# w_o and w_down with the tokens on the partitions, in a two-layer hybrid trunk kernel

## Chip, core and metric

One core of one Trainium2 chip. The metric is the device time of one execution in microseconds (us), median of three runs. The engines are TensorE (PE in the profile, its weight loads PEld), VectorE (DVE), ScalarE (ACT), GpSimd (POOL) and SyncE (SP), whose queue issues most DMA transfers.

## What is computed

One step of a trunk of two layers over 640 tokens of width 1024: 128 prompt tokens (chunk 0, with the modulation vector c_ctx) and 512 sample tokens (chunks 1 to 4, with c). Cut to what the change touches:

```python
h = rms_norm(x, g_pre1) * (1 + sc1) + sh1
parts = split(h @ w_in)                     # conv mixer, attention, DeltaNet, gates
ya, yb, yc = conv(parts) @ w_pa, attention(parts) @ w_pb, deltanet(parts) @ w_pc
mix = (ga * ya + gb * yb + gc * yc) @ w_o
x = x + gt1 * rms_norm(mix, g_post1)
h2 = rms_norm(x, g_pre2) * (1 + sc2) + sh2
ffn = (silu(h2 @ w_gate) * (h2 @ w_up)) @ w_down      # 2816 wide, 22 blocks of 128
x = x + gt2 * rms_norm(ffn, g_post2)
```

rms_norm divides by the root of the mean square over the 1024 features; scale, shift and gate are one vector each for prompt and sample tokens. Everything is fp32.

## The kernel before

All activations lie with the features on the partitions: x is eight tiles of 128x640 (block k of 128 features), and a product takes a 128x128 block of the weights as the stationary operand and 320 tokens (a half) as the moving one. For precision each fp32 operand is split into a high and a low part of the type fp32r, and a linear layer is three products per block (mm3, L362 to L365): high x high, high x low, low x high. Weight blocks come by SP into raw tiles of 128x4x128 (256 KB) and are split by ACT (a CAST, L94) and DVE (a subtraction, L95). linear (L394) streams a column block's weights for both halves; lin_half (L384) does one half with blocks that are kept.

The order of each engine's instructions is set by a scheduler at build time: a priority that follows the program's text, and free slots of the tile pools. Generators that are woven into each other (run, weave, L1196 to L1222) say which streams share a stretch. A stretch that cannot be interleaved is a joint: the norm after w_o, before the FFN, and the norm after w_down, before the next layer's input projection, since a norm needs all 1024 features of a token.

The joints are made by lin_res (L463 to L511). It does two column blocks by linear and keeps the weights of the last six (KEEP), so that half 0 of the tokens is finished ahead of half 1. For each block, sumsq (L141) squares the result on ACT and adds it up on DVE, and ACT multiplies by gate x gain (L479); after the last, half_rstd (L154) sums over the partitions by a product with a matrix of ones on PE (L157), and DVE multiplies by the factor (L496) and adds x (L497), which is read again from DRAM (xd, stored feature-wise by store_x, L459). Then prenorm_half (L192) does the same sums for the next norm and prenorm_apply (L168) makes the two fp32r parts of the next input: an ACT operation or cast for the high part (L183, L188) and a DVE operation for the low one (L184). That last half is run as a side stream in the lead (group, L410): the first five column blocks of the next stage, whose weights are ready ahead. w_down is cut in two: fill_down (L1223) does its first F1 = 14 of 22 blocks while the rest of the FFN goes on, into the tiles pt; lin_res adds the rest.

At the start load_x (L201) reads each chunk of 128 tokens with the tokens on the partitions and transposes it on PE (L211, copies L213); x's sums of squares are made by prenorm_sum, while PE does w_mod's first products (mod_mm, L271) from 16 + 16 tiles that load_first (L241) fetches. At the end out_half (L1228) transposes x back (L1236), copies it (L1237) and stores it (L1238).

## Time and profile before

| | |
|---|---|
| median of 3 runs | 2765.67 us (2762.79 to 2771.64) |
| profiled execution | 2771.84 us, span 2769.8 us |
| mean granted clock of TensorE | 0.99 |
| PE busy | 2704.1 us, 98% |
| PEld busy | 2585.7 us, 93% |
| DVE busy | 1564.8 us, 56% |
| ACT busy | 1256.1 us, 45% |
| DMA | 288.15 MB, 104 GB/s in the mean |
| 40 slices of 69 us | PE at 9 tenths or more in 38 of them, 7 in the first, 8 in the last |

The span runs from the first instruction to the end of the last transfer; the execution's own time is 2 us longer. Busy times are sums over instructions, and a product that waits in PE's pipeline counts as busy, so the start-to-start interval is what a product costs. The chain of waits goes back from the end to what released each step, and says which engine a shorter time must come from.

### The profile page before, as it was taken

The page shows a single profiled execution, that of the slowest core. Times are in us where ns is not written, and L with a number is a line of the kernel's source. Part 1 is how long each engine was busy: PE and PEld are TensorE (multiplying, and loading weights), DVE is VectorE, ACT ScalarE, POOL GpSimd, SP SyncE. Part 2 cuts the span into 40 slices and gives each one's busy share as a digit, 9 for nine tenths or more (in the row PEclk, how much of TensorE's full clock was granted, in tenths as well). Part 3 has the DMA queues.
Part 4 walks back from the last instruction along what each step waited for, and adds up shares of the span by engine and source line. Part 5 has one row for each costly group of instructions (what it writes and reads, how often), then busy time and mean ns, then how long its engine had stood idle before and what let it go on. Part 6 is the DMA issues. An engine that isn't in the chain of part 4 may idle for free.

```text
span 2769.8 us, 49615 instructions
## 1 busy us (share of the span) xinstructions
PE 2704.1 (98%) x19706; PEld 2585.7 (93%) x19706; DVE 1564.8 (56%) x3385; ACT 1256.1 (45%) x2863; POOL 26.6 (1%) x147
## 2 busy tenths in 40 slices
PE   7999999999999999999999999999999999999998
PEld 4899999999898999999989999999999999999997
DVE  4686575477743744224476865754777465442344
ACT  4533554466534633223455345544655364332343
POOL 0000000000000000000000000000000000000001
PEclk9999999999999999999999999999999999999999
DMA  8552355433564344444532323433233432222241
GB/s 241 74 77 54 81 91 109 84 67 96 162 165 152 123 133 150 128 154 146 171 89 62 71 50 86 96 87 88 66 96 120 130 97 83 77 71 75 81 120 60
DMA packets 387511, 288.15 MB, mean 104 GB/s; under 512 B 18666, under 2 KB 348112, under 8 KB 387280
## 3 DMA queue, kind: packets, MB, share of 16 engines
q1 hardware_dynamic: 387280, 285.00, 39.3%
q8 instruction: 154, 2.52, 0.4%
q14 instruction: 77, 0.63, 0.1%
HBM read 251.86 MB, written 33.07 MB: 103 GB/s over the span
## 4 chain that ended last, share of the span: by engine, by line
PE 82%; DVE 7%; DMA 5%; ACT 3%; issue 1%; SPq 0%; POOL 0%; DVEq 0%; ACTq 0%; POOLq 0%
PE l L363 23%; PE l L364 22%; PE l L365 22%; DMA wm<-in_w_mod_dram 1%; PE pm L324 1%; DMA wraw<-in_w_in_dram 1%; DMA rowb<-gd 1%; PE ptT L770 1%; PE po L780 1%; PE po L782 1%; PE scan L1068 1%; PE sco L363 1%; PE po L781 1%; DVE Tt L987 1%; PE scan L1076 1%
## 5 line engine op out<-in xcount | busy, mean ns | idle before, releaser
L94 ACT CAST whi<-wraw 128x512 fp32r<-128x512 f32 (+1 forms) x540 | 332.1, 616 | 837.1 <-PE l L364 786.6
L95 DVE TENSOR_TENSOR wlo<-wraw,whi 128x512 fp32r<-128x512 f32 (+1 forms) x540 | 367.3, 682 | 529.8 <-ACT whi L94 510.0
L363 PE MATMUL l<-hh,whi 128*128 128x320 f32 x1856 | 590.0, 318 | 5.7 <-ACT padc L858 3.3
L364 PE MATMUL l<-hl,whi 128*128 128x320 f32 x1856 | 583.5, 314 | 0.0
L365 PE MATMUL l<-hh,wlo 128*128 128x320 f32 x1856 | 582.7, 314 | 0.0
L363 PE MATMUL l<-h2h,whi 128*128 128x320 f32 x1248 | 387.4, 310 | 0.0
L364 PE MATMUL l<-h2l,whi 128*128 128x320 f32 x1248 | 385.3, 309 | 0.0
L365 PE MATMUL l<-h2h,wlo 128*128 128x320 f32 x1248 | 385.3, 309 | 0.0
L363 PEld LDWEIGHTS l<-hh,whi 128*128 128x128 f32 x1856 | 352.6, 190 | 9.3 <-ACT padc L858 3.5
L364 PEld LDWEIGHTS l<-hl,whi 128*128 128x128 f32 x1856 | 352.5, 190 | 2.0
L365 PEld LDWEIGHTS l<-hh,wlo 128*128 128x128 f32 x1856 | 352.7, 190 | 1.0
L363 PEld LDWEIGHTS l<-h2h,whi 128*128 128x128 f32 x1248 | 234.6, 188 | 7.0 <-ACT fs L427 3.1
L364 PEld LDWEIGHTS l<-h2l,whi 128*128 128x128 f32 x1248 | 234.6, 188 | 0.0
L365 PEld LDWEIGHTS l<-h2h,wlo 128*128 128x128 f32 x1248 | 234.6, 188 | 0.0
L363 PE MATMUL l<-ah,whi 128*128 128x320 f32 x544 | 169.0, 311 | 0.0
L364 PE MATMUL l<-al,whi 128*128 128x320 f32 x544 | 168.0, 309 | 0.0
L365 PE MATMUL l<-ah,wlo 128*128 128x320 f32 x544 | 167.9, 309 | 0.0
L363 PE MATMUL l<-rsh,whi 128*128 128x320 f32 x384 | 119.7, 315 | 0.0
L365 PE MATMUL l<-rsh,wlo 128*128 128x320 f32 x384 | 118.4, 310 | 0.0
L364 PE MATMUL l<-rsl,whi 128*128 128x320 f32 x384 | 118.3, 312 | 0.0
L363 PEld LDWEIGHTS l<-ah,whi 128*128 128x128 f32 x544 | 102.2, 188 | 2.2 <-issue 1.3
L364 PEld LDWEIGHTS l<-al,whi 128*128 128x128 f32 x544 | 102.3, 188 | 0.0
(427 smaller groups left out, 5310.3 us busy)
## 6 DMA issues: line engine op xcount, KB each, us to landing
wraw<-in_w_in_dram SPq DMA_DIRECT2D x256, 256.0 KB
wm<-in_w_mod_dram SPq DMA_DIRECT2D x80, 512.0 KB
wraw<-in_w_gate_dram SPq DMA_DIRECT2D x88, 256.0 KB
...
```

Of the source, the lines that this page charges most:

```text
L94: A.copy(hi, src)
L95: V.tensor_sub(lo, src, hi.bitcast(F32))
L324: T.matmul(pm[32 * u:32 * u + 2, 0:256], lhsT=sc[:, k, :], rhs=w[:, u * 256:(u + 1) * 256], start=(n == 0), stop=(n == KD - 1))
L363: T.matmul(out, lhsT=wh, rhs=ah, start=first, stop=False)
L364: T.matmul(out, lhsT=wh, rhs=al, start=False, stop=False)
L365: T.matmul(out, lhsT=wl, rhs=ah, start=False, stop=last)
L770: T.transpose(pt[:, i, q * P:(q + 1) * P], sm_[q][:, kt * P:(kt + 1) * P], ident)
L780: T.matmul(po, lhsT=vh, rhs=th, start=(kt == 0), stop=False)
L781: T.matmul(po, lhsT=vl, rhs=th, start=False, stop=False)
L782: T.matmul(po, lhsT=vh, rhs=tl, start=False, stop=(kt == 4))
L987: V.tensor_add(Tt[:, j + 1:32, 0:j], Tt[:, j + 1:32, 0:j], tv)
L1068: T.matmul(pst[:, 1, :], lhsT=XT[h, d][:, c, :], rhs=r, start=True, stop=True)
```

## The change

w_o and the second part of w_down are computed by nat_res with the tokens on the partitions: the stationary operand is now a 128x128 block of activations (128 features, one chunk of 128 tokens) and the moving one a row block of the weights, 128x512 (wrow: one transfer of 2 KB per partition). A layer is done in two groups of 512 columns. nat_stream does the first for all five chunks, k block by k block, in five banks of PSUM; the second group's split weight rows are kept meanwhile and then used chunk by chunk: chunks 0, 1, 2, then 3 and 4 interleaved. Now a token's features lie along the free axis: the sum of squares is an ACT operation with an accumulated output (sqsum), the factor a 128x1 column (tok_rstd), gate x gain is a row broadcast to all partitions (gr, made once per layer and stored in DRAM), and the residual one DVE operation. x is kept in DRAM token-wise (xd) and stored by ACT's queue. For the next stage x must come back to features on the partitions: the norm's factor is put on the diagonal of a 128x128 matrix (diag), and a full fp32 product of x's block with it transposes and scales at once (pre_t); gain and shift, four by ACT and four by DVE, the CAST of 128x8x128 and the subtraction follow. rest() does this for chunks 3 and 4 within the lead. Lead weights are split ahead in the second group (ahead). load_x uses the same diagonal products in place of transposes, and the output of the last layer is stored as it is, without transposes. fill_down uses nat_stream for both column groups; F1 is 15; the rope table lies in two C slots; the two fp32r halves of an input are two tiles of 128x8x640 (hpair).

The core of the diff:

```diff
     def load_x(c):
         xn = sb.tile([P, D], F32, tag="E", name="xn", bufs=3)
-        src = I["x_prompt"][0] if c == 0 else I["x_sample"][0, (c - 1) * P:c * P]
-        SY.dma_start(out=xn, in_=src)
+        SY.dma_start(out=xn, in_=xin(c))
         if c == 0:
             SY.dma_start(out=rows2[0:8], in_=vrow(I["c"][0]))
             SY.dma_start(out=rows2[8:16], in_=vrow(I["c_ctx"]))
+        st = small("st0", (P, 2), 3)
+        for g in range(2):
+            sqsum(st[:, g:g + 1], q4(xn[:, g * 512:(g + 1) * 512]))
+        tok_rstd(st)
+        dg = diag(st[:, 0:1])
         for g in range(2):
             pt = bank("xt")
             for j in range(4):
-                T.transpose(pt[:, j * P:(j + 1) * P], xn[:, (4 * g + j) * P:(4 * g + j + 1) * P], ident)
+                T.matmul(pt[:, j * P:(j + 1) * P], lhsT=xn[:, (4 * g + j) * P:(4 * g + j + 1) * P], rhs=dg, start=True, stop=True)
             for j in range(4):
-                (A.copy if j % 2 else V.tensor_copy)(xs[4 * g + j][:, c * P:(c + 1) * P], pt[:, j * P:(j + 1) * P])
+                (A.copy if j % 2 else V.tensor_copy)(xs[4 * g + j][:, TS[c]], pt[:, j * P:(j + 1) * P])
...
+        pt = bank("gr")
+        T.transpose(pt[0:16, 0:P], gsc[l][g[0]].rearrange("p k s -> p (k s)"), ident)
+        gr = half("gr")[0:16, 0:P]
+        A.copy(gr, pt[0:16, 0:P])
+        A.dma_start(out=gsd[l, g[0]].rearrange("k s p -> (k s) p"), in_=gr)
...
+    def wrow(srcw, k, g, keep=None):
+        raw = sb.tile([P, 4, P], F32, tag="wr", name="wraw", bufs=NWR)
+        SY.dma_start(out=raw.rearrange("p a b -> p (a b)"), in_=srcw[k * P:(k + 1) * P, g * 512:(g + 1) * 512])
+        hi, lo = wsplit(raw, [P, 4, P], keep)
+        return hi.rearrange("p a b -> p (a b)"), lo.rearrange("p a b -> p (a b)")
+    def mmn(out, act, c, wh, wl, first, last):
+        ah, al = act
+        T.matmul(out, lhsT=ah[:, TS[c]], rhs=wh, start=first, stop=False)
+        T.matmul(out, lhsT=ah[:, TS[c]], rhs=wl, start=False, stop=False)
+        T.matmul(out, lhsT=al[:, TS[c]], rhs=wh, start=False, stop=last)
...
+    def nat_stream(srcw, acts, g, ev):
+        pbs = [bank("nl"), bank("nl")] + [lbank() for _ in range(3)]
+        for k, a in enumerate(acts):
+            wh, wl = wrow(srcw, k, g)
+            for c in range(5):
+                mmn(pbs[c], a, c, wh, wl, k == 0, k == len(acts) - 1)
+                if k == len(acts) - 1:
+                    ev(c, pbs[c])
+            yield 3.2
...
-    def lin_res(srcw, acts, ys, gs, keeps, part, after, xe, end=False):
...
...
+    def nat_res(srcw, acts, gd_, xsrc, ydst, part, X, L, nrm, side=iter(()), ahead=iter(())):
...
+        def post(c, g, pb):
+            src = q4(pb)
+            if part:
+                src = u[c, g]
+                V.tensor_add(src, src, q4(pb))
+            else:
+                u[c, g] = ptile(c, g)
+            sqsum(st[:, c, g:g + 1], src)
+            V.tensor_mul(u[c, g], src, gr[int(c == 0)][g])
+            if g:
+                tok_rstd(st[:, c, 0:2])
+        def post_x(c):
+            for g in range(2):
+                V.scalar_tensor_tensor(out=u[c, g], in0=u[c, g], scalar=st[:, c, 0:1], in1=xt[c][:, 4 * g:4 * g + 4, :],
+                                       op0=ALU.mult, op1=ALU.add)
+                if nrm is None:
+                    SY.dma_start(out=q4(ydst(c))[:, 4 * g:4 * g + 4], in_=u[c, g])
+            if nrm is not None:
+                for g in range(2):
+                    sqsum(st[:, c, 2 + g:3 + g], u[c, g])
+                for g in range(2):
+                    A.dma_start(out=q4(ydst(c))[:, 4 * g:4 * g + 4], in_=u[c, g])
+            load_xt(c + 2)
+        def pre(c):
+            tok_rstd(st[:, c, 2:4])
+            dg[c] = diag(st[:, c, 2:3])
+        def pre_t(c):
+            gs, sh = nrm
+            s = int(c == 0)
+            for g in range(2):
+                pt = bank("xt")
+                for j in range(4):
+                    T.matmul(pt[:, j * P:(j + 1) * P], lhsT=u[c, g][:, j, :], rhs=dg[c], start=True, stop=True)
+                f = ft[:, 4 * g:4 * g + 4]
+                for j in range(4):
+                    k = 4 * g + j
+                    if j % 2:
+                        A.activation(f[:, j], pt[:, j * P:(j + 1) * P], AF.Identity, scale=gs[:, k, s:s + 1],
+                                     bias=sh[:, k, s:s + 1])
+                    else:
+                        V.tensor_scalar(out=f[:, j], in0=pt[:, j * P:(j + 1) * P], scalar1=gs[:, k, s:s + 1],
+                                        scalar2=sh[:, k, s:s + 1], op0=ALU.mult, op1=ALU.add)
+            A.copy(X[:, :, TS[c]], ft)
+            V.tensor_sub(L[:, :, TS[c]], ft, X[:, :, TS[c]].bitcast(F32))
...
+        kept = []
+        for k, _ in enumerate(nat_stream(srcw, acts, 0, lambda c, pb: post(c, 0, pb))):
+            if k == 1:
+                load_gr()
+            kept.append(wrow(srcw, k, 1, "C"))
             next(side, None)
-        return side
+            if k == len(acts) - 2:
+                drain(side)
+        load_xt(0)
+        load_xt(1)
+        if nrm is not None:
+            ft = sb.tile([P, KD, P], F32, tag="E", name="f", bufs=3)
+        K = range(len(acts))
+        def prod(pb, c, ks):
+            for k in ks:
+                mmn(pb, acts[k], c, *kept[k], k == 0, k == len(acts) - 1)
+        if nrm is None:
+            for c in range(5):
+                pb = lbank()
+                prod(pb, c, K)
+                post(c, 1, pb)
+                post_x(c)
+            return iter(())
+        for c in range(3):
+            pb = lbank()
+            if c == 2:
+                prod(pb, c, K[:6])
+                pre_t(0)
+                prod(pb, c, K[6:])
+            else:
+                prod(pb, c, K)
+            post(c, 1, pb)
+            if c:
+                pre(c - 1)
+            post_x(c)
+        pbs = [lbank(), lbank()]
+        for k in K:
+            for c in (3, 4):
+                prod(pbs[c - 3], c, (k,))
+            if k == 1:
+                pre(2)
+            if k == 2:
+                pre_t(1)
+            if k == 5:
+                pre_t(2)
+            if k in (1, 2, 4, 5):
+                next(ahead, None)
+        for c in (3, 4):
+            post(c, 1, pbs[c - 3])
+        post_x(3)
+        def rest():
+            pre(3)
+            post_x(4)
+            drain(ahead)
+            yield
+            pre_t(3)
+            pre(4)
+            yield
+            pre_t(4)
+        return rest()
...
     def fill_down(l, acts, part):
-        for m in range(KD):
-            linear(I["w_down"][l, 0:F1 * P, m * P:(m + 1) * P], acts, copy_ev(part[m]))
-            yield 0.8 * len(acts)
```

What moves, on three queues. On PE, at the end of layer 0's w_o and the beginning of the FFN's lead (l is a bank of PSUM, mh and ml the two parts of mix, wkh and wkl those of kept weights, h2h and h2l those of the FFN's input, pt the new x). Before:

```order
L363 MATMUL l<-mh_9808,whi 128x320
L364 MATMUL l<-ml_9809,whi 128x320
L365 MATMUL l<-mh_9808,wlo 128x320
L157 MATMUL ln<-acc,ones 128x320
L363 MATMUL l<-h2h_9872,wkh 128x320
L157 MATMUL ln<-sqt,ones 128x320
L364 MATMUL l<-h2l_9873,wkh 128x320
L365 MATMUL l<-h2h_9872,wkl 128x320
```

And with the change:

```order
L378 MATMUL l<-wkh,ml_9447 128x512
L518 MATMUL xt<-diag,pt 128x128 x8
L376 MATMUL l<-wkh,mh_9608 128x512
L377 MATMUL l<-wkl,mh_9608 128x512
L378 MATMUL l<-wkh,ml_9609 128x512
...
L378 MATMUL l<-wkh,ml_9759 128x512
L237 MATMUL ct<-ident,rows 128x128
L345 MATMUL l<-h2h,wkh 128x320 x3
L346 MATMUL l<-h2l,wkh 128x320
L347 MATMUL l<-h2h,wkl 128x320
```

The products with ones and their places between the lead's products are gone; chunk 2's eight products with the diagonal stand 12 products ahead of the end of w_o, and the lead begins right behind it.

On ACT at the same place with the change (L150 is a sum of squares, L125 and L126 make a factor, L523 is gain and shift from the bank xt, L89 a weight's CAST, L528 the CAST of a chunk's input):

```order
L150 ACTIVATE trash,st<-l 128x512
L523 ACTIVATE f<-xt,modT_290,gsc_2_294 128x128 x2
L125 ACTIVATE st<-st,eps 128x1
L89 CAST wkh<-wraw 128x512
L523 ACTIVATE f<-xt,modT_290,gsc_2_294 128x128
L126 ACTIVATE st<-st 128x1
L150 ACTIVATE trash,st<-l 128x512
L528 CAST h2h<-f 128x8x128
```

The two L150 read the banks of chunks 3 and 4, and chunk 2's L528 stands behind both. At the joint to layer 1 its place is the other one:

```order
L528 CAST hh<-f 128x8x128
L89 CAST wkh<-wraw 128x512 x2
L523 ACTIVATE f<-xt,modT_291,gsc_0_296 128x128
L89 CAST wkh<-wraw 128x512
L523 ACTIVATE f<-xt,modT_291,gsc_0_296 128x128 x3
L528 CAST hh<-f 128x8x128
L150 ACTIVATE trash,st<-pt 128x512 x2
L89 CAST whi<-wraw 128x512
```

There the CAST stands ahead of both sums.

On SP at the start (xn is a chunk of x, three buffers; wm a tile of w_mod). Before:

```order
L204 DMA xn<-in_x_sample_dram 128x1024 x4
L245 DMA wm_196<-in_w_mod_dram 128x512
L123 DMA rows<-in_b_mod_dram 48x128
L245 DMA wm_200<-in_w_mod_dram 128x512
```

And with the change:

```order
L175 DMA xn<-in_x_sample_dram 128x1024 x2
L118 DMA rows<-in_b_mod_dram 48x128
...
L122 DMA rows<-in_dn_conv_w_dram 36x128
L175 DMA xn<-in_x_sample_dram 128x1024
L221 DMA wm_239<-in_w_mod_dram 128x512
L221 DMA wm_243<-in_w_mod_dram 128x512
L175 DMA xn<-in_x_sample_dram 128x1024
L221 DMA wm_246<-in_w_mod_dram 128x512
```

The small loads moved ahead, and the last two loads of x stand among w_mod's.

## Rows read from the trace of the kernel before

**Rows 1.** The page, parts 1 (busy us, share, instructions) and 4 (chain, by engine).

```profile
PE 2704.1 (98%) x19706; PEld 2585.7 (93%) x19706; DVE 1564.8 (56%) x3385; ACT 1256.1 (45%) x2863; POOL 26.6 (1%) x147
...
PE 82%; DVE 7%; DMA 5%; ACT 3%; issue 1%; SPq 0%; POOL 0%; DVEq 0%; ACTq 0%; POOLq 0%
```

**Rows 2.** Timeline of PE, FFN: start us, us, engine line op out<-in [idle before].

```profile
1299.80 0.31 PE L365 MATMUL l<-h2h,wlo 128*128 128x320 f32 x1
...
1300.68 0.31 PE L365 MATMUL l<-h2h,wlo 128*128 128x320 f32 x1
```

**Rows 3.** Timeline of PE, attention's values, 256 columns.

```profile
523.78 0.28 PE L640 MATMUL vn<-wkl,hh 128*128 128x256 f32 x1
...
524.96 0.28 PE L641 MATMUL vn<-wkh,hl 128*128 128x256 f32 x1
```

**Rows 4.** Timeline of PEld, w_mod's products at the start.

```profile
45.13 0.09 PEld L272 LDWEIGHTS pm<-wm,sc 128*2 128x2 f32 x2 [0.34 <-issue]
...
48.56 0.09 PEld L272 LDWEIGHTS pm<-wm,sc 128*2 128x2 f32 x2 [0.34 <-issue]
```

**Rows 5.** Timeline of PE, fp32 products of 128 and of 320 columns.

```profile
152.09 2.40 PE L943 MATMUL kk<-dz 128*128 128x128 f32 x20
154.32 0.39 PE L879 MATMUL dqr<-onesc,dsq 128*128 128x2 f32 x3
...
906.51 0.71 PE L157 MATMUL pn<-acc,ones 128*128 128x320 f32 x2
...
907.21 0.31 PE L365 MATMUL l<-mh,wkl 128*128 128x320 f32 x1
```

**Rows 6.** Timeline of PE, start: the transposes of x.

```profile
5.33 1.94 PE L211 MATMUL xt<-ident,xn 128*128 128x128 f32 x8 [5.33 <-DMA xn<-in_x_prompt_dram]
...
13.73 1.07 PE L211 MATMUL xt<-ident,xn 128*128 128x128 f32 x8 [0.45 <-ACT sqt L148]
```

**Rows 7.** Timeline of PE, w_o to FFN, layer 0 and layer 1.

```profile
905.38 0.42 PE L363 MATMUL l<-mh,wkh 128*128 128x320 f32 x1 [1.49 <-ACT y L479]
...
2299.16 0.56 PE L363 MATMUL l<-h2h,wkh 128*128 128x320 f32 x2 [1.22 <-ACT h2h L188]
```

**Rows 8.** The page, part 5: the weight split.

```profile
L94 ACT CAST whi<-wraw 128x512 fp32r<-128x512 f32 (+1 forms) x540 | 332.1, 616 | 837.1 <-PE l L364 786.6
L95 DVE TENSOR_TENSOR wlo<-wraw,whi 128x512 fp32r<-128x512 f32 (+1 forms) x540 | 367.3, 682 | 529.8 <-ACT whi L94 510.0
```

**Rows 9.** Timeline of ACT, a 128x128 operation that accumulates.

```profile
99.73 0.30 ACT L932 ACTIVATE ksq<-kn 128x128 f32<-128x128 f32 x1
...
99.93 0.19 ACT L932 ACTIVATION_READ_ACCUMULATOR ksq<-kn 128x1 f32 x1
```

**Rows 10.** Windows, w_down to layer 1: us, busy by engine, PEclk, DMA share, GB/s.

```profile
1422.00:1450.00 28.00, 21.88 (x140) 18.11 (x139) 23.55 (x57) 18.96 (x47) 0.00 (x0) 0.89 0.59 154
1450.00:1457.00 7.00, 6.30 (x33) 6.28 (x34) 6.83 (x16) 4.00 (x8) 0.00 (x0) 0.71 0.24 54
```

**Rows 11.** Timeline of PE, w_down to layer 1.

```profile
1445.39 0.81 PE L157 MATMUL pn<-acc,ones 128*128 128x320 f32 x2 [1.45 <-DVE acc L152]
...
1450.70 1.17 PE L363 MATMUL l<-hh,wkh 128*128 128x320 f32 x3 [4.15 <-ACT hh L188]
```

**Rows 12.** Timeline of PE, last stage and tail.

```profile
2731.26 0.33 PE L1236 MATMUL yt<-ident,pt 128*128 128x128 f32 x1 [1.30 <-DVE pt L497]
...
2752.50 0.31 PE L365 MATMUL l<-ah,wlo 128*128 128x320 f32 x1
...
2758.57 1.88 PE L1236 MATMUL yt<-ident,pt 128*128 128x128 f32 x6 [3.87 <-DVE pt L497]
```

**Rows 13.** Timeline of DVE, the last copy.

```profile
2765.01 0.69 DVE L1237 COPY yo<-yt 128x512 f32<-128x512 f32 x1 [1.64 <-PE yt L1236]
```

**Rows 14.** Timeline of SP, start.

```profile
10.28 0.42 SPq L245 DMA_DIRECT2D wm<-in_w_mod_dram  x1
```

**Rows 15.** Windows, start, columns as in rows 10.

```profile
40.00:50.00 10.00, 9.94 (x37) 2.50 (x36) 0.27 (x1) 1.85 (x3) 0.17 (x3) 0.96 0.96 331
```

236 lines of the change are left out of this document (95 added, 141 removed).

## The prediction

> **What bounds the kernel now.** I read the page's part 1 first. TensorE is busy for 2704.1 of 2769.8 us, and the chain of waits gives PE 82% of the span and DVE 7% [rows 1]. A view by stage then has to say where the other 66 us lie, and whether a busy PE does needful work. So a change is worth the time by which it shortens PE's own stream, plus the holes of that stream that it closes, less those it opens. I went through PE's timeline for every idle time over 0.15 us in the stages that the diff touches. A measurement of this kernel can tell about 0.3% (8 us) from no change. The profiled execution took 2771.84 us, 6 above the median of 2765.67; every term is a difference within that execution, and I put the sum onto the median.
>
> **A. The products of w_o and w_down.** In steady stretches a 128x320 product starts every 0.1467 us: six intervals between 1299.80 and 1300.68 [rows 2]. The old form has (8 + 22) k blocks x 8 column blocks x 2 halves x 3 products x 2 layers = 2880 of them, 422.5 us. The new form has 30 k blocks x 5 chunks x 2 column groups x 3 x 2 = 1800 of 512 columns. No such product of the fp32r kind with 128 weight columns is in this trace. The 256-column ones start every 0.118 us, ten intervals from 523.78 to 524.96 [rows 3]. At 2.4 GHz 320 columns are 133.3 ns and 256 are 106.7, so the excess is 13.4 and 11.3 ns: it grows with the columns, but less than they do. In full proportion 512 columns take 0.2347 us; with a fixed excess of 12.4 ns, 0.2257. I take the middle, 0.230: 414 us, **-8**. The ends are 0 and -16. A farther end is w_mod's product, whose weights are two columns wide: its pairs of weight loads come every 0.429 us, eight intervals from 45.13 to 48.56, so one pass of 512 columns takes 0.2145 [rows 4]. That would be 386 us, -36; since its weight load is much smaller I keep it for a rival.
>
> **B. Full fp32 products on PE.** A 128x128 fp32 product takes 0.223 us (ten, recorded as x20, from 152.09 to 154.32); a product with ones of 128x320 takes 0.55 (0.70 from 906.51 to 907.21, less one product of 0.147 that stands between) [rows 5]. The change removes 20 of the latter in the stream (24 in all, two each in the start and the tail), -11. It adds 3 joints x 5 chunks x 8 = 120 transpositions with a diagonal, +26.7, and two small transposes per layer for the gains, +0.4. It removes the 16 transposes of the last stage that lie ahead of the tail, at 0.124 each (eight from 13.73 to the next row's start, 14.72 [rows 6]), -2. Together **+14**, all of it PE's own time; nothing hides it. Here a rule speaks against the change: the Trainium skill, page Perfetto Trace Analysis, section Transposes, wants a transposition done as a transpose and not as a standard matmul. The rows agree, 0.124 against 0.223; by the rule 12 of the 26.7 us would be saved, but the factor would then have to be applied by DVE or ACT.
>
> **C. From w_o to the FFN, twice.** Before, PE waits at 905.38 (1.49 us) and 5.65 us later (1.30) for ACT's y, and at the lead of layer 1 at 2299.16 (1.22, for ACT's h2h) [rows 7]. The same two stand in layer 1 (1.46, 1.27), and smaller ones bring it to 4.6 us in layer 0 and 4.1 in layer 1. They go with lin_res. What is late next: PE reaches the lead's first product right after chunk 4's last w_o product, and it needs chunk 2's columns of X. On ACT that CAST stands behind the sums of chunks 3 and 4, and chunk 4's sum can only start when PE has finished. I cost 0.23 (last product) + 0.62 (Square, as a 128x512 cast) + 0.19 (reading the accumulator) + 1.1 (CAST of 128x1024) and, for the low part that the fourth product needs, 1.3 on DVE, with some 0.6 of small operations and a weight split between them: 4 to 4.5 us [rows 8, 9]. I add 0.9 for a clock that may fall in such a hole, as below. Twice 5.4 less 8.7: **+2**, ends -8 (the wait is covered) and +8 (it is twice as long). The lead's own rest (chunks 3 and 4) is covered by the lead's first items, half of whose columns need only chunks 0 to 2.
>
> **D. From w_down to layer 1.** From 1422 to 1450 PE is busy for 21.88 of 28 us, and from 1450 to 1457 for 6.30 of 7 at a granted clock of 0.71 [rows 10]: 6.8 us idle, with the two holes of 1.45 and 4.15 us at 1445.39 and 1450.70, where products with ones and then the cast of hh are awaited [rows 11]. After a hole of this size the granted clock is at half (1.2 GHz) for a while; two such stretches cost some 2.7 us. Of these 9.5 us the new order leaves about 2.5: there chunk 2's CAST stands ahead of the later sums, so PE waits about 1.6 us, plus 0.9 of clock. **-7**, ends -9.5 and +3.
>
> **E. Last stage and tail.** PE waits three times for DVE's pt, 1.30 us at 2731.26 and 0.45 and 0.59 after it: -2.3. After the last product (2752.50) come two pairs of products with ones, the residual by halves, a wait of 3.87 us at 2758.57, 24 transposes [rows 12], copies, of which the last ends at 2765.70 [rows 13], and 4.1 us of output DMA to the span's end at 2769.8: 17.3 us. After: product 0.23, partial sum added on DVE 0.68, Square and accumulator 0.81, three small ones 0.7, two residual operations 1.36 (no more than the 0.68 of a tensor operation each [rows 8]), then the same 4.1 of DMA: 7.9. **-11.7** in all, ends -9 and -13.
>
> **F. The start.** Chunk 0 arrives at 5.33 us, and PE transposes at once [rows 6]. After the change two sums, the factor and the diagonal come first, 2.5 us, and each product takes twice the time of a transpose. SP issues the fourth and fifth chunk's load only when one of three xn buffers is free, and w_mod's loads are queued behind that wait: the first was issued at 10.28 [rows 14] and comes some 4 us later, into a stretch where DMA is busy for 0.96 and PE waits for it [rows 15]. The eight stores of x (2.6 MB) that followed in the same queue are gone, as are 16 Squares with their DVE additions in exchange for 10 sums, which gives back about 2. **+2**, ends -3 and +6.
>
> **Costed at nothing.** In the first column group both groups' weight rows are fetched and split: 512 KB for each k block of 15 products, 3.45 us, or 152 GB/s; the stretch from 40 to 50 us moved 331 [rows 15]. Two splits per 3.45 us are 1.25 us of ACT and 1.36 of DVE [rows 8]. If a row of weights comes late there, PE waits at its k block: one or two waits of 1 us a layer, within the ends of C. The residual's loads (five of 512 KB per pass) and the gains' broadcasts stand in SP's queue behind weight rows that are due earlier, and are needed 28 us later. The stores of x go to ACT's queue, 10 issues per joint, counted in rival 3. The larger first part of w_down (15 blocks for 14) only moves products, and the rope table in other slots leaves attention's order on PE as it was.
>
> **Sum:** -8 + 14 + 2 - 7 - 11.7 + 2 = -9: 2765.7 - 9 = **2757 us**. The bulk cancels: the wide products pay for half of the diagonals, and the gain is the tail's.
>
> **The rivals.**
> (1) *The wide product runs as w_mod's does.* At 0.2145 us per 512 columns A is -36 in place of -8, and the time 2729. For it: that row is the only 512-column pass in the trace. Against: 13.4 ns of excess at 320 columns and 11.3 at 256. The Trainium skill, page TensorE: Matmul & The Clock Gate, section Back-to-back issue gap, gives N/2.4 + 2.5 ns at the fast clock, 216 ns for 512 columns; it would also give 136 ns at 320, where the trace has 147, so the trace does not agree with it for this data type.
> (2) *The joints give nothing back.* D keeps its holes and the start costs its upper end: the order on ACT differs, but every stage there still runs sum, factor, transposition, cast one after the other. D +0, F +4: sum 0, 2766. For it: the hole of 4.15 us was such a chain too.
> (3) *ACT becomes the bound in the second column group* (slower). From the first post there to the lead, ACT has eleven sums (0.81), twelve gain-and-shift operations (0.3), three CASTs (1.1), eight weight splits (0.62), some fourteen small ones (0.2) and six DMA issues (0.4 each, as SP's [rows 14]): 26 us by these rows, in 28 us of PE. A chunk's chain from its last product to its diagonal is about 5.2 us, and PE reaches its transposition after 42 products, 9.7 us. Once ACT is over 4.5 us behind, PE stands at each of the three transpositions. At 3 us each, with the last wait of C and half clock after it, a joint costs about 8 more than forecast: 24 for three, so +15, 2781. For it: 26 of 28 leaves little. Against: in the order, the first transposition stands behind the second chunk, so a delay of one sum doesn't reach PE.
> That the change doesn't do what it says can be left out: in its order PE has the 512-wide products, and attention's products in the order of before.
>
> **How the numbers follow.** The forecast has 0.48, and about a quarter of its spread (2748 to 2766) lies within 0.3%; rival 1 has 0.12, rival 2 0.20, rival 3 0.20. Faster: 0.36 + 0.12 = 0.48. Same: 0.12 + 0.20 = 0.32. Slower: 0.20. The range leaves out the far half of rival 1 and over half of rival 3: 2735 to 2776.
>
> **What would show it.** Right: intervals of 0.226 to 0.235 us between 128x512 products; a hole of 4 to 5 us ahead of each FFN lead with ACT's h2h named, 1.6 us ahead of layer 1's; 8 us from the last product to the span's end; the first w_mod load issued at about 14 us. Wrong: intervals near 0.215 (rival 1), idle rows at the transpositions with the diagonal named (rival 3), or a shifted middle part, which nothing here expects.

## The result, and the profile after

The changed kernel takes **2793.98 us** (median of 4 runs, 2788.12 to 2799.29), the kernel before beside it 2766.66: a ratio of 1.0102, interval 1.0086 to 1.0118. Forecast were 2757 us and, for slower by over 0.3%, a chance of 0.2; the time lies outside the range. The profiled execution took 2788.12 us with a span of 2786.3, against 2771.84 and 2769.8, so the two traces show 16.5 of the 27 us. The other 11 lie in which executions were profiled: the changed kernel's is the fastest of its four, 6 below their median, and the one of before lies 5 above its median. The changed kernel's four stand in the order of their mean granted clock (0.991, 0.990, 0.988 and 0.986 for 2788.12, 2790.16, 2797.81 and 2799.29 us). A later run, before_32k, has the same instructions as the kernel before and was profiled at 2760.66 us; its trace has 25.0 us at 1.2 GHz in the record of the granted clock, and that of before 52.8; the spans differ by 11.2 us. One execution of a later kernel, of gate_rows_after, took 4003 us at a mean granted clock of 0.61 and is left out of its median.

Parts 1, 3 and 4 of the changed kernel's page, beside [rows 1]:

```profile
PE 2704.6 (97%) x18822; PEld 2518.3 (90%) x18822; DVE 1517.2 (54%) x3235; ACT 1218.3 (44%) x2817; POOL 17.9 (1%) x139
...
q1 hardware_dynamic: 343472, 278.70, 43.2%
...
PE 81%; DMA 8%; DVE 6%; ACT 3%; issue 2%; SPq 0%; DVEq 0%; POOL 0%; ACTq 0%; POOLq 0%
```

PE is as busy as before and the span longer; in the chain of waits DMA has risen from 5 to 8%. The next row of the same chain tells which DMA: the loads of w_in's blocks, which had 1% before.

```profile
PE l L345 18%; PE l L346 17%; PE l L347 17%; DMA wraw<-in_w_in_dram 4%; PE l L377 3%; PE l L376 3%; PE l L378 3%; PE nl L376 1%; PE nl L377 1%; PE nl L378 1%; DMA rowb<-gd 1%; PE pm L299 1%; DMA wm<-in_w_mod_dram 1%; PE ptT L858 1%; DVE wlo L90 1%
```

The first products of each stage in the timelines of PE cut the span into eight pieces (us). The forecast is split by the same pieces: of A, 4/15 go to the w_o's and 11/15 to the w_down's; of B's 16 us at the joints a third goes to each, and its -2 to the last stage. The last column takes the faster trace, before_32k, in place of before.

| piece | before | after | difference | forecast | against before_32k |
|---|---|---|---|---|---|
| start, to the first kk product of layer 0 | 100.8 | 111.3 | +10.5 | +2 (F) | +10.1 |
| mixers, to w_o | 748.8 | 745.4 | -3.4 | 0 | +1.5 |
| w_o, to the FFN's lead | 68.9 | 72.6 | +3.7 | +5 (A, B, C) | +4.6 |
| FFN and layer 1's lead, to its first kk | 561.0 | 574.9 | +13.9 | -4.5 (A, B, D) | +13.5 |
| mixers of layer 1, to w_o | 736.2 | 739.1 | +2.9 | 0 | +8.3 |
| w_o, to the FFN's lead | 62.8 | 65.1 | +2.3 | +5 (A, B, C) | +2.5 |
| FFN, to the last product | 474.0 | 470.1 | -3.9 | -7 (A, B, E) | -3.4 |
| last product to the end | 17.3 | 7.9 | -9.4 | -9.4 (E) | -9.4 |

By the first two traces two pieces hold the whole miss: the start and the way from w_down to layer 1. Against before_32k the pieces add up to 27.8 us, all of the difference of the medians, and layer 1's mixers are a third one with 8.3 us: the trace of before has 13.7 us at 1.2 GHz in each layer's mixers, before_32k 3.4 and none, and that hid this loss.

**The wide products** (A) in PE's timeline, [rows 2, 3]:

```profile
1435.01 0.39 PE L378 MATMUL l<-wkh,al 128*128 128x512 f32 x1
...
1437.32 0.39 PE L376 MATMUL l<-wkh,ah 128*128 128x512 f32 x1
1437.55 1.95 PE L518 MATMUL xt<-diag,pt 128*128 128x128 f32 x16
```

Ten products start in the 2.31 us from 1435.01 to 1437.32, 0.231 each. Eight products with the diagonal, recorded as x16, follow.

**w_o to the FFN** (C), the same view, [rows 7]: in layer 0

```profile
929.36 0.71 PE L345 MATMUL l<-h2h,wkh 128*128 128x320 f32 x3 [3.68 <-ACT h2h L528]
930.62 0.63 PE L346 MATMUL l<-h2l,wkh 128*128 128x320 f32 x1 [0.56 <-DVE h2l L529]
```

and in layer 1

```profile
2308.39 0.70 PE L345 MATMUL l<-h2h,wkh 128*128 128x320 f32 x3 [3.44 <-ACT h2h L528]
```

One hole per joint with h2h named, 3.7 and 3.4 us, and 0.56 behind the first: 4 to 4.5 were forecast.

**w_down to layer 1** (D), [rows 11]:

```profile
1446.37 1.17 PE L345 MATMUL l<-hh,wkh 128*128 128x320 f32 x3 [5.72 <-ACT hh L528]
...
1457.94 1.16 PE L518 MATMUL xt<-diag,p 128*128 128x128 f32 x8 [1.22 <-DVE diag L160]
...
1465.72 1.53 PE L518 MATMUL xt<-diag,p 128*128 128x128 f32 x6 [2.35 <-DVE diag L160]
```

Here 1.6 us were forecast, and 5.72 stand there; two more holes follow at transpositions of chunks 3 and 4, with the diagonal named. ACT's timeline ahead of the first:

```profile
1439.26 0.62 ACT L89 CAST wkh<-wraw 128x512 fp32r<-128x512 f32 x1 [0.23 <-DMA wraw<-in_w_in_dram]
1441.38 0.62 ACT L89 CAST wkh<-wraw 128x512 fp32r<-128x512 f32 x1 [1.50 <-DMA wraw<-in_w_in_dram]
1441.90 0.45 ACT L523 ACTIVATE f<-xt,modT,gsc 128x128 f32<-128x128 f32 x1
1443.08 0.62 ACT L89 CAST wkh<-wraw 128x512 fp32r<-128x512 f32 x1 [0.73 <-DMA wraw<-in_w_in_dram]
1443.61 0.80 ACT L523 ACTIVATE f<-xt,modT,gsc 128x128 f32<-128x128 f32 x2
1444.78 0.46 ACT L523 ACTIVATE f<-xt,modT,gsc 128x128 f32<-128x128 f32 x1 [0.38 <-DVE f L526]
1445.27 1.04 ACT L528 CAST hh<-f 128x1024 fp32r<-128x1024 f32 x1
```

hh of chunk 2, the cast that PE waits for (L528), can start at 1445.27. Its gain-and-shift operations (L523) stand among three casts of lead weights (wkh, L89), and each of these waits for its load, 2.46 us in all. How much of the hole these waits make, by_rows_after will tell below. The windows of the same time, before (columns as in [rows 10]) and after:

```profile
1425.00:1480.00 55.00, 48.95 (x339) 43.99 (x339) 40.66 (x89) 34.35 (x83) 0.00 (x0) 0.91 0.34 87
```

```profile
1425.00:1480.00 55.00, 43.70 (x268) 38.37 (x267) 30.54 (x61) 30.47 (x81) 1.17 (x11) 0.91 0.75 107
```

DMA is busy for 0.75 of this stretch in place of 0.34. The prediction priced no load of this stretch.

**The start** (F), in SP's timeline, [rows 14]:

```profile
11.68 0.35 SPq L175 DMA_DIRECT2D xn<-in_x_sample_dram  x1
12.07 0.90 SPq L221 DMA_DIRECT2D wm<-in_w_mod_dram  x2
14.29 0.33 SPq L175 DMA_DIRECT2D xn<-in_x_sample_dram  x1
14.66 2.33 SPq L221 DMA_DIRECT2D wm<-in_w_mod_dram  x5
```

and in PE's:

```profile
18.13 3.35 PE L187 MATMUL xt<-diag,xn 128*128 128x128 f32 x16 [2.13 <-DVE diag L160]
23.21 1.05 PE L187 MATMUL xt<-diag,xn 128*128 128x128 f32 x7 [1.73 <-DVE diag L160]
```

The first w_mod load comes at 12.07 and the next five from 14.66, each behind a load of x that waits for a buffer. PE waits 3.9 us for diagonals within the 40 transpositions. In the whole piece PE's idle time has grown by 5.9 us, 2.5 of them ahead of the first transposition, and the time at 1.2 GHz, in the trace's record of the granted clock, from 6.8 to 20.5 us; by estimate half of these 13.7 us is lost.

**The tail** (E), all engines, [rows 12, 13]:

```profile
2778.47 0.40 PE L378 MATMUL l<-wkh,al 128*128 128x512 f32 x1
2778.90 0.69 DVE L487 TENSOR_TENSOR pt<-pt,l 128x512 f32<-128x512 f32 x1 [0.64 <-PE l L378]
...
2782.41 0.74 DVE L497 SCALAR_TENSOR_TENSOR pt<-pt,st,xt 128x512 f32<-128x512 f32 x1
...
2783.18 0.33 SPq L500 DMA_DIRECT2D out_dram<-pt  x1
```

From the start of the last product to the span's end it takes 7.9 us; 7.9 were forecast.

**The loads of w_in.** The queue's row of the DMA view for 480 us of layer 1's mixers, before (from 1520) and after (from 1545): packets, MB, share of 16 engines.

```profile
q1 hardware_dynamic: 60736, 36.84, 31.6%
```

```profile
q1 hardware_dynamic: 62194, 38.85, 49.7%
```

share x 16 x 480 us / packets gives 40 ns for the mean packet of this queue before and 61 after. In the same stretch of layer 0 (from 120 and 130) it is 54 and 52. Most of these packets have 512 bytes; those alone, counted in the traces over the whole of layer 1's mixers, take 36 ns in the mean before and 58 after. Their median is 27 ns in both: the long ones among them have become more: 7% took over 60 ns before, 18% after. The weights and the issuing queue are the same, and their order nearly so. Nothing in the diff speaks of this, and the prediction did not look for it.

### The profile page after: what moved, and what is told of

It is laid out like the page before. It is cut to its first block, busy times and chain, and to the rows that moved or that the text cites. A ratio compares the mean times of both kernels' runs of the same rounds, so it can differ in the third digit from the quotient of the medians.

```text
span 2786.3 us, 47586 instructions
## 1 busy us (share of the span) xinstructions
PE 2704.6 (97%) x18822; PEld 2518.3 (90%) x18822; DVE 1517.2 (54%) x3235; ACT 1218.3 (44%) x2817; POOL 17.9 (1%) x139
## 4 chain that ended last, share of the span: by engine, by line
PE 81%; DMA 8%; DVE 6%; ACT 3%; issue 2%; SPq 0%; DVEq 0%; POOL 0%; ACTq 0%; POOLq 0%
PE l L345 18%; PE l L346 17%; PE l L347 17%; DMA wraw<-in_w_in_dram 4%; PE l L377 3%; PE l L376 3%; PE l L378 3%; PE nl L376 1%; PE nl L377 1%; PE nl L378 1%; DMA rowb<-gd 1%; PE pm L299 1%; DMA wm<-in_w_mod_dram 1%; PE ptT L858 1%; DVE wlo L90 1%
## 5 line engine op out<-in xcount | busy, mean ns | idle before, releaser
L89 ACT CAST whi<-wraw 128x512 fp32r<-128x512 f32 x542 | 336.6, 621 | 884.3 <-PE l L346 605.6
L90 DVE TENSOR_TENSOR wlo<-wraw,whi 128x512 fp32r<-128x512 f32 x542 | 373.2, 690 | 562.9 <-ACT whi L89 554.2
L376 PE MATMUL l<-whi,ah 128*128 128x512 f32 x222 | 87.7, 395 | 0.0
L378 PE MATMUL l<-whi,al 128*128 128x512 f32 x222 | 87.4, 394 | 0.0
L377 PE MATMUL l<-wlo,ah 128*128 128x512 f32 x222 | 87.4, 394 | 0.0
L813 ACT ACTIVATE p<-sco,nb,rq 128x320 f32<-128x320 f32 x128 | 77.5, 614 | 21.2 <-DVE nb L806 20.5
L1265 DVE TENSOR_TENSOR fs<-fs,l 128x320 f32<-128x320 f32 x88 | 42.7, 488 | 79.9 <-PE l L347 79.9
```

Source lines behind the costliest of these rows:

```text
L89: A.copy(hi, src)
L90: V.tensor_sub(lo, src, hi.bitcast(F32))
L376: T.matmul(out, lhsT=ah[:, TS[c]], rhs=wh, start=first, stop=False)
L377: T.matmul(out, lhsT=ah[:, TS[c]], rhs=wl, start=False, stop=False)
L378: T.matmul(out, lhsT=al[:, TS[c]], rhs=wh, start=False, stop=last)
L813: A.activation(p[:, o_:o_ + w], x, AF.Exp, scale=rc, bias=nb[:, 0:1], accum_out=s[:, i:i + 1])
```

## The experiments

Theories at the start: the start's and the joints' order of loads and casts makes the holes; against it, the diagonal products or ACT's own load (rival 3) do. Later: the slow packets of w_in. Each ratio is to the kernel before as measured beside it, with its 95% interval. Code is cut where a diff has "...".

**again**: the changed kernel unchanged, to see what of its profile repeats.

> The changed kernel itself, unaltered. Its first profile stands 16.5 us of span above the profile of before, its median 27 above. Theory P (places): the loss sits in the start (+7 us by the beginning of the convolution branch of layer 0) and in the hole ahead of layer 1's lead (5.7 us on ACT's cast), and both stand again in this profile to within 1 us; the rest of the 27 differs from execution to execution. Theory Q (transfers): weights land late at scattered places after the change, since the DMA engines were busy for 44.0% in place of 39.3% for the same bytes; then the start and the hole differ by over 2 us between the two profiles, and other holes of 2 to 4 us stand at other places. Ratio 1.008 to 1.012 by both.

Measured: 2798.58 us, 1.0121 (1.0101 to 1.0142). The holes of the joints come again in its timeline (5.58 us ahead of layer 1's lead, 3.56 and 3.43 ahead of the FFN's), so they are the schedule's and not one execution's. The start does not repeat so well: it takes 113.4 us for 111.3, and a hole for DVE's zz near 90 us has 5.95 where 3.06 stood, as theory Q had it.

**start_slots**: chunks 3 and 4 of x are loaded into other tiles, so that no load on SP waits for a buffer.

```diff
-        xn = sb.tile([P, D], F32, tag="E", name="xn", bufs=3)
-        SY.dma_start(out=xn, in_=xin(c))
+        if c > 2:
+            xh = [(small("p2", (P, 4, P), 2) if c == 3 else sb.tile([P, 4, P], F32, tag="wr", name="wraw", bufs=NWR)) for _ in range(2)]
+            for g in range(2):
+                SY.dma_start(out=xh[g], in_=q4(xin(c)[:, g * 512:(g + 1) * 512]))
...
```

> Chunks 3 and 4 of x are loaded into other buffers (the two p2 tiles and two raw weight tiles), so SP waits for no xn buffer and w_mod's first load is issued at about 6 to 8 us instead of 12. Theory S1 (the queue): the loss of the start was these waits; w_mod's products end 3 to 5 us earlier, and the time falls by 3 to 6 us against the changed kernel. Rival S2 (the diagonal chain on ACT and DVE, or the bandwidth of the 8 MB that the start must load): the products with w_mod end within 1.5 us of where they did and the time stays within 2 us.

Measured: 2789.83 us, 1.0090 (1.0075 to 1.0105). The first lead product starts 0.6 us earlier than before the change, no longer 4.3 later; but by the first kk product 8.5 us are lost. The timeline of all engines shows where:

```profile
84.43 0.62 ACT L89 CAST whi<-wraw 128x512 fp32r<-128x512 f32 x1 [1.98 <-DMA wraw<-in_w_in_dram]
...
85.08 0.69 DVE L90 TENSOR_TENSOR wlo<-wraw,whi 128x512 fp32r<-128x512 f32 x1 [1.91 <-ACT whi L89]
85.69 0.48 DVE L443 COPY zz<-l 128x320 f32<-128x320 f32 x1
...
86.23 0.41 PE L351 MATMUL l<-hh,wkh 128*128 128x320 f32 x1 [4.08 <-DVE zz L443]
```

ACT's cast waits for a load of w_in, DVE's subtraction for the cast, zz stands behind the subtraction on DVE, and PE waits 4.08 us for zz. What the start gives is taken again by loads.

**transpose_scaled**: DVE multiplies by the factor, and PE transposes with the identity, in all joints.

```diff
-            dg[c] = diag(st[:, c, 2:3])
+            for g in range(2):
+                V.tensor_scalar_mul(ft[:, 4 * g:4 * g + 4], u[c, g], st[:, c, 2:3])
...
-                    T.matmul(pt[:, j * P:(j + 1) * P], lhsT=u[c, g][:, j, :], rhs=dg[c], start=True, stop=True)
+                    T.transpose(pt[:, j * P:(j + 1) * P], ft[:, 4 * g + j], ident)
...
-            if k == 1:
-                pre(2)
             if k == 2:
                 pre_t(1)
+                pre(2)
```

Since the scaled rows go through the tile f (ft), chunk 2's scaling also moves behind chunk 1's transposition.

> At the three joints DVE scales each chunk's rows by the norm factor (two operations of 128x512) and PE transposes them with the identity, in place of the product with a diagonal; the start keeps its diagonals. Theory B (PE's own time): 120 blocks at 0.11 in place of 0.223 us are 13 us of PE; the time falls by 9 to 13 against the changed kernel. Rival B2 (the chain): DVE is over half busy at the joints, the scaling puts about 1 us more between the factor and PE at each chunk, the holes ahead of the leads grow by 1 to 3 us each, and the time falls by 4 to 8 at most.

Measured: 2796.61 us, 1.0107 (1.0090 to 1.0123), no gain, where both theories had one, though 120 products of 0.223 became transposes of 0.124 [rows 5, 6], 12 us of PE. In PE's timeline from w_down to layer 1 the wait has gone to the scaled operand:

```profile
1445.32 1.97 PE L519 MATMUL xt<-ident,f 128*128 128x128 f32 x8 [5.05 <-DVE f L511]
1451.28 1.17 PE L345 MATMUL l<-hh,wkh 128*128 128x320 f32 x3 [3.99 <-ACT hh L529]
...
1474.69 1.97 PE L519 MATMUL xt<-ident,f 128*128 128x128 f32 x8 [6.40 <-DVE f L511]
```

15.4 us of holes up to 1480, in place of 11.2 (the three above, and 1.07 and 0.85 behind them). So the diagonals' price is not what is missing: PE's stream is shorter, and the chain ahead of it longer. How much of that the scaling makes and how much chunk 2's later place, the run does not tell apart.

**ahead_less**: two steps of lead weights in the second column group in place of four.

```diff
-            if k in (1, 2, 4, 5):
+            if k in (1, 2):
```

> Fewer of the next stage's weights are split ahead in the second column group: two of the side stream's steps instead of four (at layer 1's joint the first block alone), the others in the lead's own side stream. Theory D1 (ACT's queue): the hole of 5.7 us ahead of layer 1's lead comes from four weight casts that wait for their loads ahead of chunk 2's gain and shift; with two of them behind it the hole falls below 3.5 us, the time by 2 to 5. Rival D2 (the chunk's own chain): sum, factor, diagonal, transposition and cast set it, the hole stays at 5 to 6 us. If the lead then waits for weights instead, its products show idle rows that name wkh, and nothing is won.

Measured: 2789.52 us, 1.0089 (1.0073 to 1.0105). The holes ahead of the FFN's leads fall (from 3.68 to 1.83 us and from 3.44 to 1.94 for the first of each). From w_down to layer 1 they grow:

```profile
1442.75 1.62 PE L345 MATMUL l<-hh,wkh 128*128 128x320 f32 x3 [4.11 <-DVE wkl L90]
...
1474.01 0.64 PE L345 MATMUL l<-hh,wkh 128*128 128x320 f32 x1 [8.09 <-ACT hh L528]
```

The way from w_down to layer 1 takes 575.5 us for 574.9, and what is gained lies at the FFN's leads. At layer 1 it is now a lead weight that comes late: there the loads themselves are short of time, while ahead of the FFN it was the place of the casts.

**Scratch in DRAM.** one_xd gives x one place in DRAM for all joints, as before the change; before_big_xd gives the kernel before three; one_xd_start_ahead is one_xd with start_slots and ahead_less.

```diff
-    xd = [dr.tile([5, P, D], F32, name=f"xd{i}") for i in range(2 * DEPTH - 1)]
+    xd = [dr.tile([5, P, D], F32, name="xd")] * (2 * DEPTH - 1)
```

> One token-wise x in DRAM (2.6 MB) in place of three, each chunk being read before it is stored again, so the scratch in DRAM is as large as before the change. Theory H (placement): packets of 512 B, which w_in's blocks consist of, took 92 ns in the mean between 1440 and 1500 us and 69 between 1500 and 1560 after the change, against 34 and 35 before, in layer 1 alone; if this comes from where the larger scratch puts things in the memory, they fall to under 45 ns, the hole ahead of layer 1's lead falls from 5.7 to under 4 us, and the time by 6 to 15 us. Rival H2 (traffic of the kernel itself: stores of x, broadcasts, a second queue): the packets stay over 60 ns and the time within 3 us of the changed kernel.

> The kernel before with its xd in DRAM three times as large (7.9 MB), two thirds of it unused; nothing else changes. Theory H (placement): layer 1's 512 B packets take over 55 ns in the mean in place of 36, and the kernel before becomes 3 to 12 us slower. Rival H2: packets and time stay as they were (within 2 us).

> One x in DRAM, chunks 3 and 4 of x loaded into other buffers at the start, and two steps of lead weights ahead instead of four. Sum of parts (theory P and H): 6 to 15 for the packets, 5 for the start, 5 for the joints: 2775 to 2783. If the parts share a cause, less: 2783 to 2788.

Measured: one_xd 2791.29 us, 1.0097 (1.0082 to 1.0111); before_big_xd 2765.30, 0.9996 (0.9987 to 1.0004); one_xd_start_ahead 2782.50, 1.0062 (1.0045 to 1.0079). In the stretches of the queue's rows above the share stays with the kernel: 48.8% for one_xd, 32.5% for before_big_xd. The size of the scratch does not make the packets slow, so that one_xd_start_ahead's time lies in a range that counted on fast packets is luck; the start and the lead blocks together bring 8 to 11 us.

**The second queue.** stores_on_sp brings the stores of x and of the gains to SP's queue; before_one_on_act gives the kernel before one load on ACT's queue (the identity); sp_start_ahead is stores_on_sp with start_slots and ahead_less.

```diff
-                    A.dma_start(out=q4(ydst(c))[:, 4 * g:4 * g + 4], in_=u[c, g])
+                    SY.dma_start(out=q4(ydst(c))[:, 4 * g:4 * g + 4], in_=u[c, g])
...
```

> The stores of x and of the gains go by SP's queue instead of ACT's, so that the program uses one hardware DMA queue, as before the change. The larger or smaller scratch changed nothing, and layer 1's 512 B packets of w_in stayed slow (69 ns in the mean from 1500 to 1560 us, 35 before). Theory K (second queue): they fall to 34 to 40 ns, and the time falls by 8 to 15 us against the changed kernel, less what SP's waits for the stores cost at the joints (up to 5). Rival K2 (anything else): over 55 ns and within 4 us.

> The kernel before with its very first transfer (64 KB, the identity) issued by ACT's queue instead of SP's. Theory K, static form (the second queue's existence changes where things lie in the memory): layer 1's packets rise from 35 to over 55 ns, layer 0's stay at 40 to 60, time 4 to 12 us longer. Theory K, dynamic form (a queue once used slows all packets after it): layer 0's rise as well, time over 10 us longer. Rival K2: nothing changes, within 2 us.

> Stores on SP, chunks 3 and 4 of x in other buffers at the start, two steps of lead weights ahead. Theory K: 8 to 15 for the packets, 5 for the start, 5 for the joints: 2768 to 2780. Rival K2: 2785, as with the last two alone.

Measured: stores_on_sp 2792.59 us, 1.0102 (1.0087 to 1.0118), share 48.4%; before_one_on_act 2764.66, 1.0000 (0.9991 to 1.0008), 32.1%; sp_start_ahead **2778.78**, 1.0047 (1.0033 to 1.0061). The queue is not the packets' cause either: sp_start_ahead's time lies in K's range, but its packets of 512 bytes in layer 1's mixers still take 56 ns, so K has no part in it. Alone the stores bring nothing; with the other two edits 15 us go, the first holes ahead of the FFN's leads are down to 0.85 us, and what is left stands at layer 1's lead:

```profile
1437.36 1.17 PE L351 MATMUL l<-hh,wkh 128*128 128x320 f32 x3 [3.59 <-ACT hh L534]
...
1466.38 0.64 PE L351 MATMUL l<-hh,wkh 128*128 128x320 f32 x1 [4.62 <-ACT hh L534]
```

**before_32k, one_xd_padded, padded_sp_start_ahead**: the scratch of the kernel before made 32 KB larger, that of the changed kernel 5 MB larger than before's (with one place for x), and the latter with the three edits.

> The kernel before with 32 KB more in its DRAM tile xd, unused; all of its instructions stay the same. Neither 5 MB of scratch more or less nor the second queue moved layer 1's packets; what is left of a placement theory is a small shift: the changed kernel has 32 KB of new scratch (the gains). Theory H3: layer 1's 512 B packets rise from 35 to over 55 ns, the time by 4 to 12 us. Rival: nothing changes (within 2 us), and the slow packets are the changed kernel's own doing.

> The changed kernel with one x in DRAM and a pad, so that all of its scratch is exactly 5 MB larger than before the change (a size at which the kernel before kept fast packets). Theory H3: layer 1's packets fall to under 45 ns, the joint's hole from 5.6 to under 4, time 2778 to 2786. Rival: packets over 60 ns, time 2788 to 2795 as with one x and no pad.

> The padded scratch with the three edits that made 2778.8 (stores on SP, other buffers for chunks 3 and 4 at the start, two steps ahead). Theory H3: 2764 to 2772. Rival: 2775 to 2782, as without the pad.

Measured: 2765.88 us, 0.9997 (0.9987 to 1.0006), share 32.5%; 2790.66, 1.0092 (1.0074 to 1.0110), 49.0%; 2777.10, 1.0040 (1.0026 to 1.0054). Where the scratch ends plays no part.

**gate_rows_after, gate_rows_before**: in the changed kernel and in the one before, w_in's 128-column blocks are fetched from w_gate.

```diff
-        linear(I["w_in"][l, :, c0:c0 + P], cur["h"], sig_ev(sg))
+        linear(I["w_gate"][l, :, c0 // P % 22 * P:(c0 // P % 22 + 1) * P], cur["h"], sig_ev(sg))
...
```

> The changed kernel, with the 128-column blocks of w_in fetched from w_gate instead (the same sizes, the same number and size of packets, other rows in DRAM; the output is not the reference's). In the changed kernel the packets of layer 1's w_in took 50 to 90 ns, those of w_gate 28. Theory P (slow packets make the weights late and so the lead's casts): packets fall to 28 ns in both layers, the hole ahead of layer 1's lead (5.6 us) falls below 3, the waits for weights in the input projection go, and the kernel takes 2775 to 2783 us. Theory Q (order on ACT and late slots, packets beside the point): packets fall, the hole stays at 5 to 6 us, the time stays within 2788 to 2794.

> The kernel before with the same edit: its control. Its packets of w_in were at 35 to 55 ns. Both theories: the waits for weights of the first layer's input projection may shrink, 2758 to 2766 us. If it gains as much as the changed kernel with this edit, the packets are no part of the difference between the two.

Measured: **2756.68** us, 0.9970 (0.9958 to 0.9982), and **2748.79**, 0.9949 (0.9934 to 0.9965), both faster than any theory had them. The same rows of the DMA view (from 1518 and from 1498):

```profile
q1 hardware_dynamic: 61840, 38.68, 27.3%
```

```profile
q1 hardware_dynamic: 61264, 37.10, 26.1%
```

34 and 33 ns for the mean packet; those of 512 bytes take 29 in both, and 1.5% of them over 60. With fast packets in both, the change costs 8 us (by the ratios 6) and not 27: some 20 us of the slowdown come with the loads of w_in. By pieces, with before_32k for the kernel before, 7.5 of them lie in layer 1's mixers, 5 in the start and 4 on the way from w_down to layer 1. In the changed kernel's chain DMA falls from 8 to 3%, and no row of w_in's or w_gate's loads with 1% or more is left in it:

```profile
PE 89%; DVE 5%; DMA 3%; ACT 2%; issue 1%; SPq 0%; DVEq 0%; ACTq 0%
```

The hole ahead of layer 1's lead stays:

```profile
1431.88 1.17 PE L345 MATMUL l<-hh,wkh 128*128 128x320 f32 x3 [4.94 <-ACT hh L528]
```

In ACT's timeline ahead of it the casts of lead weights wait for their loads 1.41 us, and not 2.46:

```profile
1426.77 0.62 ACT L89 CAST wkh<-wraw 128x512 fp32r<-128x512 f32 x1 [0.88 <-DMA wraw<-in_w_gate_dram]
...
1428.59 0.62 ACT L89 CAST wkh<-wraw 128x512 fp32r<-128x512 f32 x1 [0.53 <-DMA wraw<-in_w_gate_dram]
```

The holes behind it up to 1480 (1.22, 2.35, 1.07 and 0.85 us in the changed kernel) shrink to 0.47. So both theories of this run hold in part: the packets carry most of the time, and not this hole.

**split_on_pool**: POOL makes the high part of the kept lead blocks.

```diff
+        if pool:
+            G.tensor_copy(hi, raw)
+            V.tensor_sub(lo, raw, hi.bitcast(F32))
```

> The changed kernel, with the high part of the kept lead blocks made by POOL in place of ACT, so that no cast that waits for a load stands ahead of a chunk's gain and shift on ACT. Theory Q1 (the place of these casts on ACT makes the hole ahead of layer 1's lead): the hole of 5.6 us falls to 2 to 3, those ahead of the FFN's leads shrink by up to 1, time 2783 to 2789 us. Theory P (the loads themselves are late): the hole stays at 4 to 6 us, with POOL's cast or DVE's subtraction of a weight block named in place of ACT's, and the time stays at 2789 to 2796 or grows, POOL being slower.

Measured: 2788.81 us, 1.0081 (1.0069 to 1.0093): within Q1's range of time, for another reason than Q1's. The hole grew to 11.79 us. In PE's timeline

```profile
1447.21 1.14 PE L349 MATMUL l<-hh,wkh 128*128 128x320 f32 x3 [11.79 <-ACT hh L532]
```

and in ACT's ahead of it

```profile
1445.50 0.62 ACT L89 CAST whi<-wraw 128x512 fp32r<-128x512 f32 x1 [4.59 <-DMA wraw<-in_w_in_dram]
1446.03 1.04 ACT L532 CAST hh<-f 128x1024 fp32r<-128x1024 f32 x1
```

The scheduler's order has the cast of another weight block, which is not a kept one, just ahead of hh's, and that cast waited 4.59 us for its load. So the run did not free ACT of such casts; but it shows in one row that a weight's cast which waits for a load can hold up the cast that PE waits for.

**by_rows_after**: a load of w_in of 512 x 128 is cut into four of 128 x 128.

```diff
+            for k in range(nk):
+                SY.dma_start(out=raw[:, k, :], in_=src[k * P:(k + 1) * P])
...
```

> The changed kernel, with each load of a w_in block of 512 rows x 128 columns cut into four loads of 128 rows, so that one load reads rows that follow each other (32,832 bytes apart) and not four rows that are 128 apart by turns. Theory O (the order in which a load walks through the rows makes the packets slow): packets of w_in fall from 50 to 90 ns to below 40 in layer 1, below 45 in layer 0, the holes of the input projection go, 2757 to 2775 us. Theory O' (any reading of w_in with 512 bytes out of rows 32,832 bytes apart is as slow): packets stay at 50 to 90 ns, four times the issues on SP's queue, 2788 to 2805 us.

Measured: 2786.43 us, 1.0071 (1.0057 to 1.0085). The DMA view's row (from 1548):

```profile
q1 hardware_dynamic: 66191, 38.79, 49.7%
```

58 ns for the mean packet, with some small ones more among them: the share is that of the changed kernel, 49.7%. The order within a load does not make them slow. The time lies between the two ranges, the packets are those of O'.

This run also shows what makes the hole ahead of layer 1's lead. It is 4.81 us, and in ACT's timeline no cast of a lead weight waits for a load between chunk 2's transposition (1443.97) and the cast hh that PE waits for; chunk 2's gain and shift waits for DVE:

```profile
1447.73 0.46 ACT L530 ACTIVATE f<-xt,modT,gsc 128x128 f32<-128x128 f32 x1 [1.76 <-DVE f L533]
...
1451.86 1.17 PE L352 MATMUL l<-hh,wkh 128*128 128x320 f32 x3 [4.81 <-ACT hh L535]
```

In that time DVE does chunk 1's subtraction (1.23 us) and weight splits (0.69 each), and ACT three casts of lead weights. So the hole stands without any wait for loads, and by this comparison those of the changed kernel add about 1 us to it.

**gate_rows_edits**: gate_rows_after with the three edits of sp_start_ahead.

> The three edits of sp_start_ahead (x's stores on SP, own tiles for the last two chunks of the start, fewer lead blocks ahead) together with w_gate's rows in place of w_in's 128-column blocks (the output is not the reference's); its control is gate_rows_before, 2748.8 us. Theory S (two causes that add up, slow packets and the order of loads at the start and the joints): the edits took 14 us off the changed kernel, the rows 37, and the control gained 17, so with both 2743 to 2750 us, no slower than the control. Theory S' (the edits only helped because they softened the slow packets): 2753 to 2758, as gate_rows_after.

Measured: **2746.16** us, 0.9930 (0.9917 to 0.9943), 2.6 us below its control (2748.79), which was measured at another time; by the ratios 5. The two causes add up, and together they are most of the miss: with both gone the change gains 3 to 5 us, where 9 were forecast. The hole ahead of layer 1's lead is 2.90 us here:

```profile
1423.29 0.76 PE L351 MATMUL l<-hh,wkh 128*128 128x320 f32 x3 [2.90 <-ACT hh L534]
```

Without w_gate's rows no version beats the kernel before; the best is padded_sp_start_ahead at 1.0040.

## Why the prediction was wrong

**A: right in kind, -5 for -8.** 0.231 to 0.232 us against 0.230: 1800 x 0.232 - 422.5 = -5. Rival 1 (0.2145) is out. The Trainium skill, page TensorE: Matmul & The Clock Gate, section Back-to-back issue gap, gives 216 ns for 512 columns as the gap of an isolated product, and 131 ns for a sustained stream; the trace agrees with neither for these fp32r products (231 ns).

**B and E: right; C: right in its holes.** Eight diagonal products take 1.70 us from 1437.55 to the next start in the row's view (1439.25), 0.21 each for 0.223; the holes ahead of the FFN's leads are those forecast, by the chain named; the tail gives back the 9.4 us it was to. C's term for the clock was too small: 0.9 us a joint, where 6.8 us at 1.2 GHz stand behind each hole in the profiled execution (from 930.0 and from 2309.0), 3.4 lost by estimate. They fall into the pieces behind: into D's, and into the last stage's, which so shows 3.9 us of 7, though its holes went as forecast.

**D failed**, by 18 of the 25 us that separate the sum from the profiled difference (+13.9 in its piece, where -4.5 were forecast; 3.4 of it are the clock behind C's hole). The step said that "chunk 2's CAST stands ahead of the later sums, so PE waits about 1.6 us". It does stand ahead of the sums. But its own gain and shift shares ACT and DVE with chunk 1's subtraction and the splits of three lead weights, which the change moved into the second group (ahead), and PE has only six products (1.4 us) left behind chunk 2's transposition. The order was read for sums and not for these; "costed at nothing" looked at the loads of the first column group alone. The same hole is 5.72, 4.94 and 4.81 us with 2.46, 1.41 and 0 us of waits for loads ahead of it (after, gate_rows_after, by_rows_after), so it is the splits' place more than the lateness of their loads; with two steps fewer ahead as well it is 2.90 (gate_rows_edits). Late loads make most of the holes behind it (5.5 us up to 1480, 0.5 with w_gate's rows). By pieces, the way costs 9.4 us more than its control with fast packets and not 13.9, and 7.5 with the three edits too. Of these 7.5, A and B are about 3.5, and the joint gives nothing back, for its old holes are 1.45 and 1.95 us in gate_rows_before:

```profile
1433.28 0.70 PE L363 MATMUL l<-hh,wkh 128*128 128x320 f32 x3 [1.95 <-ACT hh L188]
```

gate_rows_edits has 2.90 and 0.50 there. The rest is not told apart. No run moved the splits alone out of this place: split_on_pool was to and did not, and gate_rows_edits has two more edits beside it.

**F failed** by 8: +2 forecast, +10.5 in its piece. That SP's queue waits for a buffer was forecast, and the first lead product is 4.3 us late, within the step's end of +6. What the step left out are two things. The later chunks' diagonals come late as well, 3.9 us of waits. And with holes of 3.43 us at 67.48 and 3.06 at 88.65, within the products of w_in, the piece has 13.7 us more at 1.2 GHz, some 7 lost by estimate; with w_gate's rows these holes are 0.59 us and nothing over 0.3, and the time at 1.2 GHz is the 6.8 us of before. By the control 5.3 of the 10.5 are left with fast packets, and nothing with the edits (93.8 us against 94.3).

**"A shifted middle part, which nothing here expects"** came: no term had a place for the loads of w_in taking longer. The mixers of layer 1 cost 2.9 us by the two profiled executions and 8.3 against before_32k, a third of the miss that the prediction had at nothing. PE waits there 4.33 us at 1520.86, where 3.27 stood before, and 2.47 at 1777.70, where nothing over 0.6 did; with w_gate's rows the piece is as long as its control's to 0.8 us.

**Rival 3** had the sign, and its row (the diagonal named at transpositions) is there, 1.22 and 2.35 us. Its mechanism is not what decides: it had ACT busy for 26 of 28 us, and ACT is busy for 18.7 of the 28 us ahead of the lead. What it had right is that ACT's other work stands ahead of the cast that PE waits for.

**The clock.** The sum allowed for it in C and D alone, with 0.9 us a joint. The trace has more: 3.4 a joint in C, and some 7 in the start. It also moves from execution to execution: the trace of before has 27.8 us more at 1.2 GHz than that of before_32k, with the same instructions. The sum was made of differences within that execution; the sizes in B and E held all the same.
